# Four small matmul pairs of an mLSTM moved from the heads to the end of the layer, their operands kept in DRAM meanwhile

## The chip, the cores and the metric

The kernel runs on one core of a Trainium2 chip. The metric is device microseconds of one launch, as the median of 3 runs. TensorE (PE) multiplies matrices into PSUM banks, VectorE (DVE), ScalarE (ACT) and GpSimd (POOL) compute on SBUF and PSUM, SyncE (SP) issues DMAs; ACT and POOL issue some too. Each engine executes its instructions in the order in which they stand in its program; between engines semaphores order them.

## The reference

One inference step of one hybrid decoder layer, in float32: 256 prompt tokens and 8 sample tokens (264 columns in all) of width 2048. The part that the change touches is the mLSTM's memory after the prompt, per head (4 heads, key width 128, value width 256):

```python
xn = rmsnorm(x, g_mix);  z = xn @ w_in
q, k, v, logi, logf = ...                    # slices of z
h_ml, C_new, n_new, m_new = mlstm(q, k, v, logi, logf, C0, n0, m0)
# within mlstm, with w_end the weight that each token keeps at the end:
num = ... + jnp.einsum('bhts,bhsv->bhtv', qk, vc)
den = ... + jnp.sum(qk, axis=-1)
C_new = dec[..., None, None] * C + jnp.einsum('bhs,bhsd,bhsv->bhdv', w_end, kc, vc)
n_new = dec[..., None] * n + jnp.einsum('bhs,bhsd->bhd', w_end, kc)
...
x = x + jnp.concatenate([y_rg, y_ml], axis=-1) @ w_out
x = x + o @ w_xa_o                           # cross attention
x = x + (jax.nn.silu(xf @ w_ffn_gate) * (xf @ w_ffn_up)) @ w_ffn_down
y = rmsnorm(x, g_final)
```

For the prompt the old memory is zero, so C_new and n_new are one product: weighted keys (256 tokens x 128) transposed, times values with a column of ones (256 x 257, kept as 258). They are outputs only; nothing later in the layer reads them. The sample tokens have a memory of their own (input c0T, output o_sc), which is read, updated and written back.

## The kernel before

**Weights.** The main loop at the end of layer_kernel walks a list of steps, one for each column block of a weight matrix (w_in, the memory's w_k and w_v, w_out, w_q, w_o, w_gu, w_d in three parts). SP's DMAs bring a step's weights into `raw` (5 buffers of 128x1024, load_piece); ACT rounds them to fp32r and DVE subtracts, which gives a high and a low part in `w` (4 buffers, split_half). PE multiplies each 128x128 chunk three times (high by high, high by low, low by high): 48 matmuls for a step of 16 chunks, 36 in the last part of w_d, which has 12.

**Side work.** Around the weight matmuls run generators that the loop advances (pump): ml_prompt makes each head's masked scores Pm and weighted keys kw, ml_values its values vt, ml_heads the head's sums, ml_sample the update of the sample tokens' memory. A scheduler of the framework then sets each engine's order, except SP's, which is the order of the code.

**The heads.** For each head, ml_heads issues two pairs of matmuls for the output (nps), two for the new memory (cps, 128x258 in a PSUM bank) and three of one column for the denominators (dps, in the same bank behind the memory's columns). ACT copies nps, dps and cps out; cps goes into `cn`, and once all four heads are there POOL writes cn to the output o_pc.

**The sample memory.** ml_sample goes over 4 heads in 8 groups. fetch, called one group ahead, issues three DMAs on POOL's queue: the group's memory from c0T, and two reads that spread rows of a DRAM scratch (`scr`, keys and queries) over all partitions. ACT scales (`dw`), DVE updates and reduces (`ds`), and POOL writes the group to o_sc. POOL issues these in its program's order.

**The end.** The last step's evf is final(15): while PE has no more weights it issues filler matmuls (warm, rows `mm<-ones`); DVE adds the residual, ACT squares, PE sums over partitions (fin_sums, rows `ax<-ones,t`), rstd_fin computes the reciprocal root, PE spreads it to all partitions (spread, rows `ax<-ident,c`), and DVE and POOL scale the 16 blocks of y, which SP and ACT write to o_y in nine DMAs (132 KB a block).

All compute instructions go through the wrapper class Engine, so the profile shows them as line L60; they are told apart by tile names. `B` is a pool of 26 SBUF buffers; PSUM has banks `mm` and `ax`, four each.

Of the kernel before, what the change touches and what calls it, by code (L numbers as in the profile page):

```python
# [10 lines left out]
F32 = mybir.dt.float32  # L11
F32R = mybir.dt.float32r
I32 = mybir.dt.int32
AF = mybir.ActivationFunctionType
# [3 lines left out]
P = 128  # L18
D = 2048
KC = D // P  # L20
T = 256
# [3 lines left out]
H = 4  # L25
# [69 lines left out]
def layer_kernel(ctx: ExitStack, tc, xT, memT, vec, wrg, w_in, w_out, w_q, w_k, w_v, w_o,  # L95
# [3 lines left out]
    act, dve, pe = Engine(nc.scalar, price_act), Engine(nc.vector, price_dve), Engine(nc.tensor, price_pe)  # L99
    pool_e, sp = nc.gpsimd, nc.sync  # L100
# [4 lines left out]
    drm = ctx.enter_context(tc.tile_pool(name="drm", bufs=1, space=bass.MemoryType.DRAM))  # L105
# [8 lines left out]
    def nm(s):  # L114
        uid[0] += 1
        return f"{s}_{uid[0]}"

    def B(shape, dt=F32):
        return sb.tile(shape, dt, tag="B", bufs=NB, name=nm("B"))

    def tmp(w=N, tag="t"):
        t = sb.tile([P, N], F32, tag=tag, bufs=NT if tag == "t" else NL, name=nm(tag))
        return t[:, :w]
# [36 lines left out]
    fin = {}  # L160


    steps = []
# [100 lines left out]
    def halves(x):  # L264

        return x.rearrange("p (b a) -> p b a", b=2)

    def unturn(ps):

        return ps.rearrange("p (a b) -> p b a", b=2)  # L270
# [61 lines left out]
    def bank(tag="mm"):  # L332
        return psm.tile([P, 512], F32, tag=tag, bufs=4, name=nm(tag))
# [3 lines left out]
    def warm(n, w=None):  # L337

        ps = bank()
        for _ in range(n):  # L340
            pe.matmul(ps[:, :P], ones if w is None else w.to_broadcast([P, P]), ones, start=True, stop=True)
# [16 lines left out]
    def ctile(w):  # L358
        t = sb.tile([P, 16], F32, tag="c", bufs=8, name=nm("c"))
        return t[:, :w]  # L360
# [23 lines left out]
    def spread(ps, c, n=N):  # L384

        for j in range(2 if n == T else 3):
            lo, hi = (j * P, j * P + P) if j < 2 else (T, N)
            pe.matmul(ps[:, lo:hi], c[j].to_broadcast([P, P]), ident[:, P - (hi - lo):], start=True, stop=True)
# [48 lines left out]
    def rstd_fin(ps):  # L437
        v, r, t = ctile(3), ctile(3), ctile(3)
        dve.tensor_scalar(v, ps[:, :3], 1.0 / D, EPS, op0=OP.mult, op1=OP.add)
        act.activation(r, v, AF.Sqrt)  # L440
        dve.reciprocal(r, r)
        dve.tensor_mul(t, r, r)
        dve.scalar_tensor_tensor(t, t, -0.5, v, op0=OP.mult, op1=OP.mult)
        dve.scalar_tensor_tensor(r, t, 1.5, r, op0=OP.add, op1=OP.mult)
        warm(3, v[:, 0:1])
        for k in "ps", "copied":
            fin[k] = bank("ax")
            spread(fin[k], [r[:, j: j + 1] for j in range(3)])
        act.activation(rstd, fin["copied"][:, :N], AF.Copy)

    def fin_sums(ps, x, first):

        for j, w0 in enumerate(WIN):
            pe.matmul(ps[:, j: j + 1], x[:, w0: w0 + P], ones[:, 0:1], start=first and j == 0,
                      stop=not first, skip_group_check=True)
# [281 lines left out]
        return f  # L737

    hT = {}

    def ml_prompt():
        qk = ml["qk"]
# [53 lines left out]
            yield STEP  # L796

    def ml_heads():
        cn = B([P, H, 258])
        hT["t"] = Arr(8)  # L800
        hh = hT["t"]
        one = ones[:, 0:1]
        for h in range(H):
            while min(ml.get("pn", 0), ml.get("vtn", 0)) <= h:
                yield STEP
            yield STEP
            vt = ml["vt", h]
            Pm, kw = ml["w", h]
            nps = bank("ax")
            for vb in range(2):  # L810
                o = vb * T
                pe.matmul(nps[:, o: o + T], vt[:, 0, vb * P: vb * P + P], Pm[:, 0:256], start=True, stop=False)
                pe.matmul(nps[:, o + P: o + T], vt[:, 1, vb * P: vb * P + P], Pm[:, 256:384],
                          start=False, stop=True)
            cps = bank("ax")
            pe.matmul(cps[:, 0:258], kw[:, 0:P], vt[:, 0, :], start=True, stop=False)
            pe.matmul(cps[:, 0:258], kw[:, P:T], vt[:, 1, :], start=False, stop=True)
            dps = cps[:, 300:302]
            pe.matmul(dps[:, 0:1], Pm[:, 0:P], one, start=True, stop=True)
            pe.matmul(dps[:, 1:2], Pm[:, P:T], one, start=True, stop=False)  # L820
            pe.matmul(dps[:, 1:2], Pm[:, 256:384], one, start=False, stop=True)
            for vb in range(2):
                act.activation(hh(2 * h + vb)[:, 0:T], nps[:, vb * T: vb * T + T], AF.Copy)
            act.activation(den[:, 3 * h: 3 * h + 2], dps, AF.Abs)
            act.activation(cn[:, h, :], cps[:, 0:258], AF.Copy)
        pool_e.dma_start(o_pc, cn)
        yield STEP

    snew = const.tile([P, H, NS], F32, name="snew")
# [199 lines left out]
    def final(m):  # L1029

        def f(ps):
            x = xres[:, m, :]
            if m == 0:
                st["y"] = Arr(KC)
            if m < KC - 1:
                dve.tensor_add(halves(x), halves(x), unturn(ps[:, :N]))
                sumsq(acc_x, x, m == 0)
            else:
                warm(3)
                sq = tmp()  # L1040
                with tc.high_priority():
                    for b in range(2):
                        xb = halves(x)[:, b, :]
                        dve.tensor_add(xb, xb, unturn(ps[:, :N])[:, b, :])
                        act.activation(halves(sq)[:, b, :], xb, AF.Square)
                fin_sums(fin["sum"], sq, False)
            act.activation(st["y"](m), x, AF.Copy, scale=V("g_final", m))
            if m == 0:
                act.activation(warm_act, acc_x[:, 0:1], AF.Sqrt)
            elif m == KC - 2:  # L1050
                fin["sum"] = bank("ax")
                fin_sums(fin["sum"], acc_x, True)
            elif m == KC - 1:
                rstd_fin(fin["sum"])
        return f
# [380 lines left out]
    kept = ExitStack()  # L1436
    for i, (src, cols, pef, evf, need) in enumerate(steps):
        if i > 1:
            load_piece(i + LD - 1)
        if i == 7:  # L1440
            st["rg"] = side(rg_gen(), 0)
        if "pend" in need:
            with tc.high_priority(300):
                for e, x in pend:
                    e(x)
            pend = []
        for q in need:
            if q in st:
                finish(lambda: st[q].done)
        if not 4 <= i < 7:  # L1450
            with tc.high_priority(300):
                for e, x in pend:
                    e(x)
            pend = []
        now = pe.clock
        dve.clock, act.clock = max(dve.clock, now), max(act.clock, now)
        split_half(i + LS, 0)
        if i + LS < len(steps) and steps[i + LS][1] > 1024:
            split_half(i + LS, 1)
        if i == 4:  # L1460
            kept.enter_context(tc.manual_schedule(engines={mybir.EngineType.PE}))
        ps = pef(i)
        if i == 6:
            kept.close()
        if i == 1:
            with tc.issue_after(st["split"].ins):
                for c in range(8):
                    sumsq(acc_x, xres[:, c, :], c == 0)
        if i == 3:
            with tc.issue_after(st["split"].ins), tc.high_priority():  # L1470
                last_squares()
            st["rstd_x"] = Gen(norm_x())
        if evf is not None:
            pend.append((evf, ps))
        if i == 0:
            for c in range(0, 4, 2):
                load_x(sp, 12 + c, 14 + c)
                load_first(3, c)
                load_first(3, c + 1)
        else:  # L1480
            load_piece(i + LD)
        pump(pe.clock + SLACK)
        if i == 24:
            st["ng"] = side(ml_norm(), 6)
        if i == 57:
            PACE["full"] = False
        if i == 40:
            st["memg"] = side(mem_gen(), 7)
    for e, x in pend:
        e(x)  # L1490
    for lo, hi in ((0, 1), (1, 2), (2, 4), (4, 6), (6, 8), (8, 10), (10, 12), (12, 14), (14, 16)):
        for c in range(lo, hi):
            e, r = (pool_e, rstd) if c in POOLC else (dve, fin["ps"][:, :N])
            e.tensor_mul(st["y"](c), st["y"](c), r)  # L1494
        (act if lo in (1, 4, 8, 12) else sp).dma_start(o_y[:, lo:hi, :], st["y"].tile(lo // 4)[:, lo % 4: lo % 4 + hi - lo, :])


# [104 lines left out]
```

## Time and profile before

| what | value |
|---|---|
| median of 3 runs | 1456.94 us |
| all runs | 1456.13, 1456.94, 1457.64 us |
| profiled execution, time | 1455.83 us |
| profiled execution, span | 1454.1 us |
| granted TensorE clock | 0.998 |
| PE busy | 1439.2 us |
| DVE / ACT / POOL busy | 1045.1 / 794.9 / 128.3 us |
| DMA moved | 326.02 MB, mean 224 GB/s |

The profile is of one execution; the difference between its time and its span, 1.73 us, lies ahead of its first and behind its last instruction or transfer. A row of a timeline gives the start, the duration, the engine, the line, the operation, what it writes and reads, shapes, how many instructions, and in brackets the idle time before it with what ended that. Rows of windows give each engine's busy time, then the granted clock, the DMA engines' busy share and GB/s. f32 matmuls show as several instructions each.

### The profile page before, as it was taken

What the parts mean: (1) busy time and instruction counts of PE and PEld (TensorE: products, weight loads), DVE (VectorE), ACT (ScalarE), POOL (GpSimd) and SP (SyncE); (2) the same over time, 40 slices, a digit from 0 to 9 for tenths busy, and PEclk for the clock granted to TensorE, in tenths of its full rate; (3) what the DMA queues carried; (4) which work ended last, traced back from release to release, by engine and by line L of the source; (5) the groups of instructions that cost most, each with busy time, mean ns of one, the idle gap of its engine ahead of it and who ended that gap; (6) DMA issues with size and microseconds to landing.
All of it is one profiled execution on the core that took longest, in us unless ns stands there. A gap on an engine that the chain in (4) does not pass through costs nothing.

```text
span 1454.1 us, 30126 instructions
## 1 busy us (share of the span) xinstructions
PE 1439.2 (99%) x12071; PEld 1415.5 (97%) x12071; DVE 1045.1 (72%) x1999; ACT 794.9 (55%) x1279; POOL 128.3 (9%) x204
## 2 busy tenths in 40 slices
PE   9999999999999999999999999999999999999997
PEld 8999999999999999999999999999999999999997
DVE  7966797898899999987675666555665655565564
ACT  7678685666556666655544444434444443444463
POOL 0001210000124343410000000000000000000000
PEclk9999999999999999999999999999999999999999
DMA  9645896557799877955555555555555555555563
GB/s 288 234 171 179 268 363 231 177 178 271 254 344 355 340 284 297 375 172 192 197 195 194 197 193 201 190 202 190 198 194 196 196 198 194 195 197 192 172 195 112
DMA packets 99757, 326.02 MB, mean 224 GB/s; under 512 B 10944, under 2 KB 19824, under 8 KB 99616
## 3 DMA queue, kind: packets, MB, share of 16 engines
q1 hardware_dynamic: 83616, 269.84, 52.8%
q0 software_dynamic: 15136, 53.16, 10.2%
q8 instruction: 94, 1.54, 0.4%
q10 hardware_dynamic: 864, 1.09, 0.2%
q14 instruction: 47, 0.39, 0.1%
HBM read 312.78 MB, written 11.28 MB: 223 GB/s over the span
## 4 chain that ended last, share of the span: by engine, by line
PE 94%; ACT 2%; DMA 1%; DVE 1%; issue 1%; SPq 0%; POOL 0%; DVEq 0%; POOLq 0%
PE mm L60 90%; PE ax L60 5%; DMA raw<-w_in 1%; ACT B L60 1%; DVE B L60 1%; DMA B<-scr 0%; ACT w L60 0%; DVE w L60 0%; ACT L60 0%; SPq L213 0%; ACT dw L60 0%; DVE ds L60 0%; SPq L1412 0%; DMA scr<-lt 0%; ACT t L60 0%
## 5 line engine op out<-in xcount | busy, mean ns | idle before, releaser
L60 PE MATMUL mm<-B,w 128*128 128x264 f32 (+1 forms) x10960 | 1281.2, 279 | 2.5 <-DVE w L60 2.1
L60 PEld LDWEIGHTS mm<-B,w 128*128 128x128 f32 x10960 | 1260.6, 189 | 10.7 <-DVE w L60 2.4
L60 DVE TENSOR_TENSOR w<-raw,w 128x1024 fp32r<-128x1024 f32 (+1 forms) x522 | 625.4, 1200 | 312.9 <-ACT w L60 312.2
L60 ACT ACTIVATE w<-raw 128x1024 fp32r<-128x1024 f32 (+1 forms) x522 | 536.0, 1028 | 531.8 <-PE mm L60 370.8
L60 PE MATMUL mm<-w,B 128*128 128x512 f32 x384 | 86.5, 380 | 0.0
L60 PEld LDWEIGHTS mm<-w,B 128*128 128x128 f32 x384 | 70.7, 189 | 9.4
L1494 POOL TENSOR_TENSOR B<-B,rstd 128x264 f32<-128x264 f32 x4 | 2.8, 741 | 802.8 <-ACT rstd L60 802.8
L60 DVE TENSOR_TENSOR t<-mm,rstd 128x264 f32<-128x264 f32 x96 | 41.4, 432 | 28.8 <-PE mm L60 28.7
L60 DVE SCALAR_TENSOR_TENSOR B<-B,dw 128x256 f32<-128x256 f32 x128 | 52.2, 461 | 3.2 <-ACT dw L60 2.9
L60 DVE TENSOR_TENSOR xres<-xres,mm 128x264 f32<-128x264 f32 (+1 forms) x81 | 34.2, 424 | 27.2 <-PE mm L60 27.1
L60 DVE SCALAR_TENSOR_TENSOR dw<-B,qsm,dw 128x256 f32<-128x256 f32 x96 | 48.6, 512 | 0.8
L60 PE MATMUL ax<-B,B 128*128 128x256 f32 (+3 forms) x288 | 46.0, 302 | 0.8 <-DVE B L60 0.8
L1162 POOL TENSOR_TENSOR ds<-dw,ds 128x256 fp32r<-128x256 f32 x32 | 36.8, 1151 | 106.9 <-ACT ds L60 104.7
L60 PEld LDWEIGHTS ax<-B,B 128*128 128x128 f32 x288 | 39.9, 191 | 3.0 <-DVE B L60 1.0
L60 ACT ACTIVATE B<-xres,vecs 128x264 fp32r<-128x264 f32 (+1 forms) x64 | 32.1, 502 | 3.5 <-DVE xres L60 1.6
L60 ACT ACTIVATE t<-xres 128x264 f32<-128x264 f32 (+1 forms) x53 | 21.0, 409 | 16.0 <-DVE xres L60 16.0
L1151 POOL DMA_DIRECT2D B<-kcT x32 | 17.4, 544 | 122.8 <-DVE B L60 109.7
L60 DVE SCALAR_TENSOR_TENSOR B<-xres,vecs,B 128x264 fp32r<-128x264 f32 x48 | 23.3, 488 | 4.3 <-ACT B L60 4.3
L60 ACT ACTIVATE dw<-B,qsm 128x256 f32<-128x256 f32 x32 | 16.2, 507 | 16.3 <-issue 6.4
L60 ACT ACTIVATE B<-t 128x264 fp32r<-128x264 f32 (+1 forms) x60 | 24.1, 409 | 1.7 <-DVE t L60 1.5
L60 ACT ACTIVATE dw<-B,B 128x128 f32<-128x128 f32 x64 | 20.9, 390 | 7.1 <-DMA B<-scr 6.3
L60 ACT ACTIVATE dw<-ax,dw 128x256 f32<-128x256 f32 x32 | 15.0, 470 | 17.7 <-DVE dw L60 14.0
(172 smaller groups left out, 691.2 us busy)
## 6 DMA issues: line engine op xcount, KB each, us to landing
raw<-w_gu SPq DMA_DIRECT2D x176, 512.0 KB, 3.6
raw<-w_d SPq DMA_DIRECT2D x80, 512.0 KB, 3.7
raw<-w_in SPq DMA_DIRECT2D x74, 512.0 KB, 5.2
raw<-w_out SPq DMA_DIRECT2D x32, 512.0 KB, 3.8
B<-kcT POOLq DMA_DIRECT2D x32, 512.0 KB, 8.2
raw<-w_q SPq DMA_DIRECT2D x32, 512.0 KB, 5.4
B<-vcT POOLq DMA_DIRECT2D x32, 512.0 KB, 9.1
raw<-w_k SPq DMA_DIRECT2D x32, 512.0 KB, 5.1
```

The lines of the kernel that those rows point to most:

```text
L60: return f(*a, **k)
L1151: pool_e.dma_start(kc, kcT[h, b])
L1162: pool_e.tensor_sub(ws[:, 1], acc, ws[:, 0].bitcast(F32))
L1494: e.tensor_mul(st["y"](c), st["y"](c), r)
```

## The change

The matmuls for cps leave ml_heads. In their place two POOL DMAs for each head write kw (128 KB) and vt (258 KB) to two DRAM tiles, kept_k and kept_v, and dps gets a bank of its own. ACT's four copies of cps and POOL's write of o_pc leave too.

In the last part of w_d, state_load puts eight loads on SP's queue, between weight loads, which bring keys and values back into three B buffers (a fourth takes the result). The same eight matmuls, two for each head, then stand behind the last weight matmul: the first takes the place of two of three fillers ahead of fin_sums, the next two that of the three fillers ahead of the spreads, the other five follow the spreads. ACT copies the four results (state_out), and SP writes o_pc in two halves of 258 KB, one between two writes of y and one as the last of all. PE's order is that of the code from the last step on.

```diff
@@ rstd_fin
-        warm(3, v[:, 0:1])
+        state_mm((0, 1), (1, 0))
         for k in "ps", "copied":
             fin[k] = bank("ax")
             spread(fin[k], [r[:, j: j + 1] for j in range(3)])
+        state_mm((1, 1))
         act.activation(rstd, fin["copied"][:, :N], AF.Copy)
+        state_out(0, act)
+        state_out(1, act)
+        state_mm((2, 0), (2, 1), (3, 0), (3, 1))
+        state_out(2, act)
+        state_out(3, act)
@@ ahead of ml_prompt
+    kept_k = drm.tile([H, P, T], F32, name="kept_k")
+    kept_v = drm.tile([H, P, 2, 258], F32, name="kept_v")
+
+    def state_load():
+        kb, vb, out = B([P, H, T]), [B([P, 2, 2, 258]), B([P, 2, 2, 258])], B([P, H, 258])
+        for h in range(H):
+            sp.dma_start(kb[:, h], kept_k[h])
+            sp.dma_start(vb[h // 2][:, h % 2], kept_v[h])
+        fin["state"] = kb, vb, out
+        fin["cps"] = {}
+
+    def state_mm(*parts):
+        kb, vb, out = fin["state"]
+        for h, t in parts:
+            if t == 0:
+                fin["cps"][h] = bank("ax" if h % 2 else "mm")
+            pe.matmul(fin["cps"][h][:, 0:258], kb[:, h, t * P: t * P + P], vb[h // 2][:, h % 2, t, :],
+                      start=t == 0, stop=t == 1)
+
+    def state_out(h, engine):
+        out = fin["state"][2]
+        engine.activation(out[:, h, :], fin["cps"][h][:, 0:258], AF.Copy)
@@ ml_heads
-        cn = B([P, H, 258])
...
-            cps = bank("ax")
-            pe.matmul(cps[:, 0:258], kw[:, 0:P], vt[:, 0, :], start=True, stop=False)
-            pe.matmul(cps[:, 0:258], kw[:, P:T], vt[:, 1, :], start=False, stop=True)
-            dps = cps[:, 300:302]
+            pool_e.dma_start(kept_k[h], kw)
+            pool_e.dma_start(kept_v[h], vt)
+            dps = bank("ax")[:, 0:2]
...
-            act.activation(cn[:, h, :], cps[:, 0:258], AF.Copy)
-        pool_e.dma_start(o_pc, cn)
@@ final
-                warm(3)
+                state_mm((0, 0))
+                warm(1)
...
+            elif m == 4:
+                state_load()
@@ main loop and end
+        if i == len(steps) - 1:
+            kept.enter_context(tc.manual_schedule(engines={mybir.EngineType.PE}))
...
+        if lo == 4:
+            sp.dma_start(o_pc[:, 0:2], fin["state"][2][:, 0:2])
         (act if lo in (1, 4, 8, 12) else sp).dma_start(o_y[:, lo:hi, :], ...)
+    sp.dma_start(o_pc[:, 2:4], fin["state"][2][:, 2:4])
```

Three places of the programs show what moves.

POOL, from the write of the last hidden state on, before (c0T and scr are a fetch of the sample memory, o_sc its write; scr's row stands for both halves):

```order
L587 DMA o_h<-hlast 128x72
L896 DMA o_sc<-B_1890 128x1024
L896 DMA o_sc<-B_1985 128x1024
L866 DMA B_2109<-c0T 128x1024
L870 DMA B_2110<-scr 128x512 x2
L896 DMA o_sc<-B_2109 128x1024
L866 DMA B_2320<-c0T 128x1024
```

and now:

```order
L593 DMA o_h<-hlast 128x72
L844 DMA kept_v<-B_1628 256x1x258
L843 DMA kept_k<-B_1890 128x256
L921 DMA o_sc<-B_1891 128x1024
L921 DMA o_sc<-B_1986 128x1024
L844 DMA kept_v<-B_1628 256x1x258
L843 DMA kept_k<-B_1979 128x256
L891 DMA B_2109<-c0T 128x1024
L895 DMA B_2110<-scr 128x512 x2
L843 DMA kept_k<-B_2078 128x256
L844 DMA kept_v<-B_1629 256x1x258
```

The keys and values of two heads stand ahead of the third fetch, the second head's (B_1979) directly ahead of it and behind the two o_sc; those of the third and the keys of the fourth stand ahead of the fourth fetch.

PE at the second head, before (rows of 128x258 are the new memory, rows from `ones` the denominators, mm a weight step):

```order
L60 MATMUL mm_2243<-B_149,w_2122 128x264
L60 MATMUL mm_2243<-B_148,w_2122 128x264 x2
L60 MATMUL mm_2243<-B_149,w_2122 128x264
L60 MATMUL mm_2243<-B_148,w_2122 128x264
L60 MATMUL ax_2205<-B_1626,B_1978 128x258 x2
L60 MATMUL ax_2205<-ones,B_1978 128x1 x3
L60 MATMUL mm_2243<-B_175,w_2122 128x264
```

and now:

```order
L60 MATMUL mm_2242<-B_151,w_2122 128x264
L60 MATMUL mm_2242<-B_150,w_2122 128x264 x2
L60 MATMUL mm_2242<-B_151,w_2122 128x264
L60 MATMUL mm_2242<-B_150,w_2122 128x264
L60 MATMUL ax_2207<-ones,B_1979 128x1 x3
L60 MATMUL mm_2242<-B_177,w_2122 128x264
```

The denominators' matmuls follow the weight matmuls directly; they have a bank of their own (ax_2207) instead of the end of the memory's.

PE at the end, from the last weight matmul on, before (`mm<-ones` are fillers, `ax<-ones,t` the sums, `ax<-ident,c` the spreads):

```order
L60 MATMUL mm_17732<-B_16571,w_17683 128x264
L60 MATMUL mm_17769<-ones 128x128 x3
L60 MATMUL ax_17728<-ones,t_17773 128x1 x3
L60 MATMUL mm_17791<-ones,c_17782 128x128 x3
L60 MATMUL ax_17795<-ident,c_17783 128x128 x2
L60 MATMUL ax_17795<-ident,c_17783 128x8
L60 MATMUL ax_17799<-ident,c_17783 128x128 x2
L60 MATMUL ax_17799<-ident,c_17783 128x8
```

and now, from the first instruction behind the last weight matmul (128x258 rows are the moved matmuls):

```order
L60 MATMUL mm_17779<-B_17211,B_17210 128x258
L60 MATMUL mm_17781<-ones 128x128
L60 MATMUL ax_17736<-ones,t_17783 128x1 x3
L60 MATMUL mm_17779<-B_17211,B_17210 128x258
L60 MATMUL ax_17802<-B_17211,B_17210 128x258
L60 MATMUL ax_17804<-ident,c_17793 128x128 x2
L60 MATMUL ax_17804<-ident,c_17793 128x8
L60 MATMUL ax_17808<-ident,c_17793 128x128 x2
L60 MATMUL ax_17808<-ident,c_17793 128x8
L60 MATMUL ax_17802<-B_17211,B_17210 128x258
L60 MATMUL mm_17816<-B_17212,B_17210 128x258 x2
L60 MATMUL ax_17819<-B_17212,B_17210 128x258 x2
```

Five of six fillers are gone, and of the eight moved matmuls five stand behind the spreads.

More of the change, by code (lines that the diff above doesn't have):

```diff
@@ L1490, in layer_kernel @@
         e(x)
+    kept.close()
     for lo, hi in ((0, 1), (1, 2), (2, 4), (4, 6), (6, 8), (8, 10), (10, 12), (12, 14), (14, 16)):
```

## The prediction

> **What bounds the kernel now.** I read the page first, then every wait of TensorE, then the two stretches that the change edits: the mLSTM heads (150 to 190 us) and the last 14 us.
>
> ```profile
> span 1454.1 us, 30126 instructions
> PE 1439.2 (99%) x12071; PEld 1415.5 (97%) x12071; DVE 1045.1 (72%) x1999; ACT 794.9 (55%) x1279; POOL 128.3 (9%) x204
> PEclk9999999999999999999999999999999999999999
> PE 94%; ACT 2%; DMA 1%; DVE 1%; issue 1%; SPq 0%; POOL 0%; DVEq 0%; POOLq 0%
> ```
>
> PE is busy for 1439.2 of 1454.1 us at full clock, and the chain of waits is 94% PE. A PE instruction taken out therefore shortens the run by what PE issues for it, as long as PE finds the next work ready. The other 15 us lie at the two ends, where a transfer or a short chain decides. In the heads only one wait of PE is seen, the 0.81 us in the first row below.
>
> **What is removed.** Here are PE's rows of the first two heads (start, duration, instructions). The x4 rows of 128x258 are the matmuls that leave; f32 is issued as pieces, four for a head's two matmuls.
>
> ```profile
> 154.50 1.14 PE L60 MATMUL ax<-B,B 128*128 128x258 f32 x4 [0.81 <-DVE B L60]
> 155.48 0.72 PE L60 MATMUL ax<-ones,B 128*128 128x1 f32 x6
> 165.73 1.03 PE L60 MATMUL ax<-B,B 128*128 128x258 f32 x4
> 166.60 0.72 PE L60 MATMUL ax<-ones,B 128*128 128x1 f32 x6
> ```
>
> Durations overlap, so I take start to start: 166.60 - 165.73 = 0.87 us a head. The first shows 0.98, of which I put 0.11 to the restart behind its wait. Four heads: 4 x 0.87 = **-3.48 us**. The four ACT copies and the output's DMA on POOL leave too. I cost them at nothing: ACT waits for PE in most of these gaps, so PE's work covers them. Were the cover gone, that would be worth 4 x 0.38 us (the 156.31 row below is such a copy).
>
> **What the heads add: a longer POOL queue.** Keys and values now leave by POOL DMAs, 128 + 258 KB a head, and a DMA waiting at POOL holds up what is queued behind it. Behind the second head's keys stands the third fetch of the sample state (c0T, then two halves of scr). The rows of POOL and ACT before:
>
> ```profile
> 150.54 0.54 POOL L896 DMA_DIRECT2D o_sc<-B  x1 [7.14 <-DVE ds L60]
> 151.10 0.54 POOL L866 DMA_DIRECT2D B<-c0T  x1
> 151.63 1.08 POOL L870 DMA_DIRECT2D B<-scr  x2
> 154.32 0.39 ACT L60 ACTIVATE B<-B,B 128x128 f32<-128x128 f32 x1
> 156.31 0.38 ACT L60 ACTIVATE B<-ax 128x258 f32<-128x258 f32 x1
> 161.00 1.28 ACT L60 ACTIVATE dw<-B,B 128x128 f32<-128x128 f32 x4 [0.81 <-DMA B<-scr]
> 161.72 1.07 DVE L60 SCALAR_TENSOR_TENSOR B<-B,bcs,dw 128x256 f32<-128x256 f32 x2 [0.27 <-ACT dw L60]
> 163.26 0.74 DVE L60 TENSOR_SCALAR B<-ax,gcol 128x256 f32<-128x256 f32 x2
> ```
>
> The second head's keys are finished by the ACT row at 154.32, thus at 154.71. Their DMA takes one issue slot (0.54), so the fetch starts near 155.3 instead of 151.10: 4.2 us later. It has no slack: ACT at 161.00 already waits 0.81 us for the scr half. Behind ACT stand DVE's state update (161.72) and, in DVE's order, the gate rows ending at 163.26 + 0.74 = 164.00, which free the PSUM bank that PE's second-head sums need.
>
> How much later does scr land? Not the full 4.2 us, if bandwidth rather than issue decides. Two stretches, the first scr read in the chain of waits, and the landings of all of them:
>
> ```profile
> 150.00:155.00 5.00, 4.19 (x28) 3.76 (x27) 5.00 (x20) 2.67 (x7) 2.15 (x4) 1.00 0.85 278
> 155.00:160.00 5.00, 5.00 (x44) 4.92 (x44) 3.78 (x7) 3.77 (x9) 0.00 (x0) 1.00 0.95 301
> 130.03 5.85 DMA B<-scr
> DMA to landing us min/median/max: 1.8/10.1/16.4
> ```
>
> The last two numbers of the windows are DMA share and GB/s. The engines are 85 and 95% busy, so bytes ahead of the fetch decide: 386 KB (0.395 MB) of the second head at 0.278 to 0.301 MB/us is 1.3 to 1.4 us, plus some 0.3 us of idle share that the later issue leaves unused. I take a delay d = **1.7 us**. The bounds: issued at 155.8, with the 5.85 us that the earliest scr read took, it lands at 161.7, against the 161.0 where ACT started (d = 0.7); with the whole issue delay and no help, d = 4.2.
>
> PE now comes to those sums 0.98 us earlier (head one's pieces are gone), at 165.73 - 0.98 = 164.75, and the bank is free at 164.00 + d = 165.7. It stalls 0.95 us: **+0.95**. (d = 0.7 gives no stall, d = 4.2 gives 3.45 us, all of the gain.)
>
> ```profile
> 206.04 1.21 DVE L60 TENSOR_TENSOR w<-raw,w 128x1024 fp32r<-128x1024 f32 x1
> 190.00:200.00 10.00, 10.00 (x91) 10.00 (x91) 10.00 (x44) 9.97 (x30) 1.61 (x3) 1.00 1.02 409
> 200.00:210.00 10.00, 10.00 (x92) 10.00 (x91) 10.00 (x31) 7.62 (x16) 1.60 (x3) 1.00 0.87 334
> ```
>
> From 190 to 210 us DVE is busy all the time, with weight splits like the 1.21 us one among the state updates, and DMA is at a share of 1.02. The four later fetches start some 2 us late, and part of PE's lead meets weights that are not split yet. Against it, 516 KB of output leaves this stretch. I take **+0.2** (0 to 1.5: none if the splits keep their lead, one 1.21 us split and a little if one fetch comes a whole DMA later).
>
> The DMA queues' rows of the window 169 to 176, in which two weight loads were issued, bear on this price:
>
> ```profile
> q0 software_dynamic: 425, 1.51, 86.9%
> q1 hardware_dynamic: 3, 0.01, 0.3%
> raw<-w_in SPq DMA_DIRECT2D x2, 512.0 KB, 12.0
> ```
>
> POOL's queue (q0) had 86.9% of the engines and the weights' queue (q1) 0.3%. So POOL's bytes are served ahead of weights and kept keys and values push weights back in full, which is why I keep an upper end of 1.5. The Trainium skill ("DMA: Bandwidth & Descriptors", "Queues, rings and completion order") says that each engine alternates between the queue rows it has work for, packet by packet; by that, weights would lose about half as much, and the +0.2 would be +0.1. The trace does not agree here.
>
> **What the last layer adds.** The eight loads (1.58 MB) are issued by SP in the last down projection. At 0.39 MB/us they need 4.0 us of all engines, where the share is
>
> ```profile
> 1410.00:1420.00 10.00, 10.00 (x92) 10.00 (x91) 6.02 (x11) 6.33 (x11) 0.00 (x0) 1.00 0.62 192
> 1430.00:1440.00 10.00, 10.00 (x92) 10.00 (x91) 4.62 (x9) 4.17 (x8) 0.00 (x0) 1.00 0.01 2
> ```
>
> 0.62, then 0.01: the weights are all in by 1430, ten microseconds ahead of PE. I cost the loads at **0**, hidden behind that lead; without it, 4.0 us.
>
> The eight matmuls go into PE's gaps at the end (the last row is the landings of y):
>
> ```profile
> 1441.56 0.83 PE L60 MATMUL mm<-ones 128*128 128x128 f32 x6
> 1442.45 0.83 PE L60 MATMUL ax<-ones,t 128*128 128x1 f32 x6
> 1443.54 0.94 PE L60 MATMUL mm<-ones,c 128*128 128x128 f32 x6 [0.25 <-DVE c L60]
> 1444.57 1.50 PE L60 MATMUL ax<-ident,c 128*128 128x128 f32 x12
> 1445.45 4.16 DVE L60 TENSOR_TENSOR B<-B,ax 128x264 f32<-128x264 f32 x12 [0.93 <-PE ax L60]
> 1445.90 4.71 SPq L1495 DMA_DIRECT2D o_y<-B  x5
> 1446.25 3.22 ACTq L1495 DMA_DIRECT2D o_y<-B  x4
> DMA to landing us min/median/max: 1.8/2.3/3.3
> ```
>
> One matmul is 0.87 / 2 = 0.435 us. The first, with one filler where three stood, has 0.89 us (1441.56 to 1442.45); two, 0.87 us, replace the fillers ahead of 1444.57; the other five stand behind the spreads (end 1446.07) and hold up nothing but their own copies, done near 1448.9. **0** on the path, or up to 0.4 if the first pieces crowd the 1442.45 row. ACT's copies of 0.38 us stand between its own y writes, 0 to 0.4 likewise.
>
> What costs is the output's 516 KB, which went out at 192 us and now goes beside y:
>
> ```profile
> 1447.00:1448.00 1.00, 0.00 (x0) 0.00 (x0) 1.00 (x4) 0.00 (x0) 1.00 (x3) 1.00 0.79 282
> 1448.00:1449.00 1.00, 0.00 (x0) 0.00 (x0) 1.00 (x4) 0.00 (x0) 1.00 (x3) 1.00 1.04 393
> 1450.00:1451.00 1.00, 0.00 (x0) 0.00 (x0) 0.00 (x0) 0.00 (x0) 0.00 (x0) 0.50 1.05 401
> 1452.00:1453.00 1.00, 0.00 (x0) 0.00 (x0) 0.00 (x0) 0.00 (x0) 0.00 (x0) 0.50 0.62 239
> ```
>
> From 1448 to 1452.6 the DMA engines are full at 0.39 to 0.40 MB/us while they drain y, after every engine has ended. 0.528 MB / 0.397 = **+1.3 us**. Below: 1.1, since 1447 has 0.2 us of share free; if the span's end were set by something else, 0. Above: 1.8, with another 0.5 us for the last write's landing (y's median less its least, 2.3 - 1.8).
>
> **Sum:** -3.48 + 0.95 + 0.2 + 0 + 1.3 = -1.03. The profiled run took 1455.83 us, 1.73 around its span, and lies 1.11 below the median of 1456.94. So 1455.83 - 1.03 = 1454.8 for a run like it, and 1456.94 - 1.03 = **1455.9** for the median.
>
> **Rivals.** *A, no stall.* If scr lands by 161.7 and the splits keep their lead, -3.48 + 1.3 = -2.2: 1454.8. For it: the landing of 5.85 us. Against: 10.1 is the median of these reads.
>
> *B, the queue at POOL decides (slower).* The place is the second head's keys ahead of the third fetch. If the fetch keeps its 4.2 us and also the 1.3 us of kept bytes, d = 5.5, the stall is 5.5 - 0.75 = 4.75, 1.27 us more than the gain; with the split's 1.5 and the tail's 1.3 that is +4.1: 1461.0. It decides from d = 4.23 on, where stall and removed work cancel. For it: ACT's 0.81 us wait shows no slack at all, and weights get no share while POOL's queue is full. Against: DMA bytes, not issue times, filled 155 to 160.
>
> *C, the tail is cheaper than its bytes.* If the span's end hangs on the last y write's landing rather than on drained bytes, the output hides: 1456.94 - 3.48 = 1453.5. Against: the engines are full to the end.
>
> *D, weights late at the end.* If the 1.58 MB come ahead of weights that PE needs, up to +4.0 - 1.03: 1459.9. Against: the ten idle microseconds at 1430.
>
> That the change does not do what it says I leave out: the matmuls do stand at the end.
>
> **Numbers.** The forecast has 0.47 (own range 1454.6 to 1457.4), A 0.16, C 0.12, B 0.20, D 0.05. A measurement here tells 0.2% (2.9 us) from no change: faster is below 1454.0, slower above 1459.9. C alone is faster, with a little of A's edge: 0.13. Slower are B and half of D: 0.22. The rest, 0.65, is no change. The range 1453.8 to 1460.2 leaves out most of C and the far part of B.
>
> **What would show it.** Right: no 128x258 rows in the heads and 0.87 us less between their neighbours; the third c0T row at POOL near 155.3 and ACT's wait for scr grown from 0.81 to some 2.5 us; one PE wait of about 1 us at the second head's sums; PE's last weight matmul 2.3 us earlier; DMA full 1.3 us longer behind it. A PE wait over 3.5 us there, or PE waits on weight splits between 180 and 220, is B. Weight waits beyond 1400 are D. A drain that is no longer is C. I am wrong altogether if PE's last weight matmul ends later than before, or the tail grows by over 2 us.

## The result, and the profile after

The changed kernel takes 1459.12 us (median of 20 runs, 1456.52 to 1462.48); the kernel before takes 1457.01 us (20 runs, 1455.88 to 1458.47). The ratio is 1.0017, 95% interval 1.001 to 1.0024: 1.5 to 3.5 us slower. The forecast was 1455.9, faster by 1.0.

The profiled execution of the changed kernel took 1461.94 us, at the upper end of its runs. Its page opens with

```profile
span 1460.2 us, 30141 instructions
PE 1442.5 (99%) x12061; PEld 1418.0 (97%) x12061; DVE 1047.2 (72%) x1999; ACT 794.4 (54%) x1279; POOL 133.7 (9%) x211
```

PE issues 10 instructions fewer than before and is still "busy" 3.3 us longer. Busy time grows without work when the clock falls, so the place to look for is one where PE first waits and then runs slowly (it will account for 1.66 of the 3.3 us). The rows of PE in the heads (start, duration, instructions, and in brackets the wait ahead of them):

```profile
153.42 0.59 PE L60 MATMUL ax<-B,ident 128*128 128x256 f32 x2
156.79 0.83 PE L60 MATMUL ax<-ones,B 128*128 128x1 f32 x6 [0.81 <-DVE B L60]
165.72 1.60 PE L60 MATMUL mm<-B,w 128*128 128x264 f32 x12
170.49 1.04 PE L60 MATMUL ax<-ones,B 128*128 128x1 f32 x6 [3.18 <-DVE B L60]
171.39 5.75 PE L60 MATMUL mm<-B,w 128*128 128x264 f32 x36
176.98 1.47 PE L60 MATMUL ax<-B,B 128*128 128x256 f32 x8
178.28 0.73 PE L60 MATMUL ax<-ones,B 128*128 128x1 f32 x6
192.09 43.11 PE L60 MATMUL mm<-B,w 128*128 128x264 f32 x381
```

The 128x258 rows are gone. At the second head's sums PE waits 3.18 us where it had not waited, and the next 36 weight pieces take 5.75 us; they had taken 4.30 (the same row before: `167.19 4.30`). The windows, with the granted clock ahead of the DMA share and GB/s, tell why:

```profile
169.00:171.00 2.00, 0.51 (x5) 0.51 (x5) 2.00 (x11) 2.00 (x6) 0.00 (x0) 0.99 0.01 4
171.00:172.00 1.00, 1.00 (x6) 1.00 (x7) 1.00 (x2) 1.00 (x4) 0.21 (x1) 0.50 0.00 0
173.00:174.00 1.00, 1.00 (x7) 1.00 (x6) 1.00 (x6) 0.46 (x2) 0.56 (x1) 0.50 0.62 156
174.00:175.00 1.00, 1.00 (x9) 1.00 (x9) 0.64 (x5) 0.59 (x1) 0.61 (x2) 0.81 0.92 291
175.00:176.00 1.00, 1.00 (x12) 1.00 (x11) 0.50 (x1) 0.47 (x1) 1.00 (x2) 1.00 0.97 383
```

Behind the wait the clock is a half from 171.0 to 174.4 us. The sums take 0.90 us start to start (170.49 to 171.39) instead of 0.59, the weights 1.45 us more: 1.76 us in all. Of these, 0.10 is the restart behind a wait, which the first head shows at full clock too (156.79 to 157.48, 0.69 us); 1.66 is the clock, a cause that no term of the forecast held.

Who made PE wait? POOL's rows, and those of ACT and DVE behind them:

```profile
152.83 0.54 POOL L921 DMA_DIRECT2D o_sc<-B  x1 [6.83 <-DVE ds L60]
153.36 0.72 POOL L844 DMA_DIRECT2D kept_v<-B  x1
157.28 0.56 POOL L843 DMA_DIRECT2D kept_k<-B  x1 [3.21 <-ACT B L60]
157.83 0.55 POOL L891 DMA_DIRECT2D B<-c0T  x1
158.36 1.08 POOL L895 DMA_DIRECT2D B<-scr  x2
```

```profile
156.60 0.39 ACT L60 ACTIVATE B<-B,B 128x128 f32<-128x128 f32 x1
167.62 1.28 ACT L60 ACTIVATE dw<-B,B 128x128 f32<-128x128 f32 x4 [5.14 <-DMA B<-scr]
169.70 0.74 DVE L60 TENSOR_SCALAR B<-ax,gcol 128x256 f32<-128x256 f32 x2
```

POOL waits 3.21 us for the second head's keys (ACT's row at 156.60) and only then issues the third fetch. ACT waits 5.14 us for scr, DVE's gate rows end at 170.44, and PE starts at 170.49. In this execution all of it runs 2.28 us later than before already ahead of the heads (153.42 against 151.14 for the same PE row). So in the times of before, the fetch starts at 157.83 - 2.28 = 155.55 instead of 151.10, and ACT gets scr at 167.62 - 2.28 = 165.34 instead of 161.00: a delay of 4.3 us, nearly the whole 4.45 us of later issue. (The second profile of the same kernel, e10 below, has 3.3 us.)

Those 2.28 us belong to that execution (e10 has 0.57): 1.8 of them come from the first scr read, for which ACT waited until 138.19 instead of 135.90, and it was issued at 130.83, ahead of the first write of keys or values (143.15).

The end: PE's last weight pieces, before

```profile
1441.14 0.58 PE L60 MATMUL mm<-B,w 128*128 128x264 f32 x3
```

and now, and the windows of the drain.

```profile
1445.45 0.58 PE L60 MATMUL mm<-B,w 128*128 128x264 f32 x3
1446.76 0.83 PE L60 MATMUL ax<-ones,t 128*128 128x1 f32 x6
1448.88 1.50 PE L60 MATMUL ax<-ident,c 128*128 128x128 f32 x12 [0.31 <-DVE c L60]
```

```profile
1451.00:1452.00 1.00, 1.00 (x6) 0.89 (x5) 1.00 (x4) 0.52 (x2) 1.00 (x2) 1.00 0.78 270
1453.00:1454.00 1.00, 0.00 (x0) 0.00 (x0) 0.92 (x3) 0.16 (x1) 0.75 (x2) 1.00 1.02 395
1457.00:1458.00 1.00, 0.00 (x0) 0.00 (x0) 0.00 (x0) 0.00 (x0) 0.00 (x0) 0.89 1.03 398
1458.00:1459.00 1.00, 0.00 (x0) 0.00 (x0) 0.00 (x0) 0.00 (x0) 0.00 (x0) 0.50 0.29 112
```

From the x3 row to the span's end it is 1460.2 - 1445.45 = 14.75 us; before it was 1454.1 - 1441.14 = 12.96. The sums and the spreads stand at the same distances as before (1.31 and 3.43 us), so the moved matmuls cost PE's path nothing; what grew, by 1.79 us, is the drain. (Counted from the last weight instruction, as the expectations below do, it is 0.31 us less: 14.44 and 12.65.)

### The profile page after: what moved, and what is told of

The parts are those of the page before. It is cut to its first block, busy times and chain, and to the rows that moved or that the text cites. A ratio compares the mean times of both kernels' runs of the same rounds, so it can differ in the third digit from the quotient of the medians.

```text
span 1460.2 us, 30141 instructions
## 1 busy us (share of the span) xinstructions
PE 1442.5 (99%) x12061; PEld 1418.0 (97%) x12061; DVE 1047.2 (72%) x1999; ACT 794.4 (54%) x1279; POOL 133.7 (9%) x211
## 4 chain that ended last, share of the span: by engine, by line
PE 68%; DVE 1%; issue 0%; ACT 0%; POOL 0%; DVEq 0%; POOLq 0%; ACTq 0%
PE mm L60 66%; PE ax L60 2%; DVE B L60 0%; DVE w L60 0%; DVE dw L60 0%; POOL ds L1190 0%; ACT w L60 0%; DVE c L60 0%; ACT dw L60 0%; ACT ds L60 0%; DVE osm L60 0%; DVEq L1613 0%; ACT t L60 0%; DVE xres L60 0%; ACT c L60 0%
```

## The experiments

Each was compared with the kernel before on the same chip; ratios are to it.

**e1, the removal alone.** From the change, the writes, the loads, the moved matmuls and o_pc are left out.

```diff
-            pool_e.dma_start(kept_k[h], kw)
-            pool_e.dma_start(kept_v[h], vt)
...
-                state_mm((0, 0))
-                warm(1)
+                warm(3)
```

> The changed kernel without its POOL writes of keys and values, without the loads and without the moved matmuls: the new memory is not computed and o_pc is not written. It prices the removal alone. Theory (POOL's queue delays the third fetch, and only that turns the gain round): the third c0T stands at POOL near its time of before, PE waits under 1 us at the second head's sums, and the run is 2.5 to 3.5 us faster than before (4 x 0.87 us). Rival (the shifted order of ACT and DVE in the heads, not POOL's queue, makes the stall): the wait of about 3 us at the second head's sums stays, and the gain is under 1 us.

Measured: 1453.12 us, ratio 0.9972 (0.9961 to 0.9984), about 4 us faster. PE's rows around the sums of the second head, and the third fetch:

```profile
165.53 0.72 PE L60 MATMUL ax<-ones,B 128*128 128x1 f32 x6
166.11 4.30 PE L60 MATMUL mm<-B,w 128*128 128x264 f32 x36
```

```profile
150.84 0.53 POOL L861 DMA_DIRECT2D B<-c0T  x1
```

No wait, full clock, the fetch in time. PE, DVE and ACT have the changed kernel's order in the heads, so that order isn't what stalls. The removal is worth what the forecast said (3.5 us lies in the interval). That this execution has no 0.81 us wait at the first head is no part of the gain: its clock had fallen earlier, near 127 us, and PE came there late (see e6).

**e2, without the end's part.** The change with its POOL writes, without loads, moved matmuls, copies and o_pc.

```diff
-            elif m == 4:
-                state_load()
...
-    sp.dma_start(o_pc[:, 2:4], fin["state"][2][:, 2:4])
```

> The changed kernel with its POOL writes of keys and values, but without the eight loads, the moved matmuls, their copies and o_pc (which is not written). Against e1 it adds the eight writes alone, against the changed kernel it lacks the tail alone. Theory: the wait of 3 us at the second head's sums and the half clock behind it are there (1.5 to 1.8 us), so it is as fast as before or up to 1.5 us slower; the changed kernel's further 1.3 to 1.8 us is the tail. Rival (the tail costs the whole 2.1 us): 2 us faster than before, like e1.

Measured: 1458.18 us, ratio 1.0012 (1.0003 to 1.002). The wait is there:

```profile
167.82 0.83 PE L60 MATMUL ax<-ones,B 128*128 128x1 f32 x6 [3.20 <-DVE B L60]
```

```profile
169.00:170.00 1.00, 1.00 (x8) 1.00 (x8) 1.00 (x5) 1.00 (x4) 0.68 (x1) 0.71 0.00 0
170.00:171.00 1.00, 1.00 (x6) 1.00 (x6) 1.00 (x7) 0.36 (x2) 0.38 (x1) 0.50 0.67 102
```

Eight POOL writes turn e1's gain of 4 us into a loss of 1.7; that is the larger part of the matter. Between e2 and the change lies the end: 0.0005 of the ratio, which is 0.7 us, with intervals that overlap, and 1.8 us by the profiles' ends (14.75 against 12.92 from the x3 row).

**e3, the writes by SP.** One word in two lines; PE, DVE and ACT keep the changed order.

```diff
-            pool_e.dma_start(kept_k[h], kw)
-            pool_e.dma_start(kept_v[h], vt)
+            sp.dma_start(kept_k[h], kw)
+            sp.dma_start(kept_v[h], vt)
```

> The whole change, with the eight writes of keys and values issued by SP instead of POOL. POOL's order is that of before; PE, DVE and ACT keep the changed kernel's order. Theory: the third fetch is issued in time, the stall at the second head's sums falls under 1 us and the clock stays up; what is left is -3.48 + 1.4 to 1.8 for the tail: 1.5 to 2.2 us faster than before. Rival (bandwidth: 386 KB a head ahead of the fetch, whoever issues it): the wait stays above 2 us and the time is no better than before. A second rival: SP waits for the second head's keys and holds the weights behind them, which shows as PE waits on the weight splits ahead of 190 us.

Measured: 1454.99 us, ratio 0.9989 (0.998 to 0.9998): 1.6 us faster than before, with all of the work done.

```profile
151.24 0.53 POOL L891 DMA_DIRECT2D B<-c0T  x1
```

```profile
160.91 1.28 ACT L60 ACTIVATE dw<-B,B 128x128 f32<-128x128 f32 x4 [0.55 <-DMA B<-scr]
```

The same bytes move in the same stretch (the first head's go out at 150.43, the second head's at 156.24) and scr comes in time; so the bytes were not the price. The read's own time varies, though: in e8, with the same writes by SP, scr came 11.67 us behind its issue instead of 9.15, and PE waited 0.55 us at the second head's sums; whether the bytes do that is not shown. PE shows no wait on weight splits there in e3: SP's own wait for the keys costs nothing.

**e4, the writes by ACT.** As e3, with ACT's queue.

```diff
+            nc.scalar.dma_start(kept_k[h], kw)
+            nc.scalar.dma_start(kept_v[h], vt)
```

> As e3, with the writes issued by ACT, right behind the instructions that make the keys and values. Theory: the third fetch is in time as in e3; eight issue slots of some 0.4 us stand in ACT's order, 3 us in all, mostly while ACT waits for the scr reads: 0.5 to 2.2 us faster than before, not better than e3. Rival: ACT's slots delay weight rounding between 142 and 160 us and PE waits for ACT there: slower than e3 by 1 us or more.

Measured: 1455.09 us, ratio 0.999 (0.9981 to 0.9998), not to be told from e3. ACT's slots cost nothing that these runs show.

**e5, only the second head by SP.**

```diff
+            kq = sp if h == 1 else pool_e
+            kq.dma_start(kept_k[h], kw)
+            kq.dma_start(kept_v[h], vt)
```

> The whole change; only the second head's keys and values are written by SP, the other three heads' by POOL as in the change. Theory (one DMA that waits at POOL ahead of the third fetch is the whole loss): the third c0T is back near 151 to 153 us, PE's wait at the second head's sums is under 1 us, the clock stays at 1.00, and the run is 1 to 2 us faster than before, as e3. Rival (the six other writes cost too, by their slots ahead of the later fetches or by their bytes): between the changed kernel and e3, no faster than before.

Measured: 1455.48 us, ratio 0.9991 (0.9982 to 1.0). The third c0T is issued at 150.68 and PE doesn't wait at the sums. Six of the eight writes may stay on POOL; the two of the second head make nearly all of the difference to the change.

**e6, PE kept busy through the wait.** The second head's output matmuls are done four times.

```diff
-            for vb in range(2):
+            for vb in (0, 1) * (4 if h == 1 else 1):
```

> The changed kernel, with the second head's output matmuls done four times over instead of once (the same result is written again): 24 more PE pieces, 3.7 us by the 1.23 us that eight take, ahead of the sums that PE waits for; 12 pieces of weight matmuls (1.43 us) come behind the sums instead of ahead of them. Theory (the half clock behind the 3.2 us wait is set off by PE's idleness): PE waits under 1.6 us there, the clock stays at 1.00, the next 36 weight pieces take 4.3 instead of 5.75 us, and the added work costs nothing: +1.43 for the pieces moved behind, -1.76 for the clock, 0.3 us faster than the changed kernel or equal to it. Rival (the clock falls there for another reason): it falls again, and the run is 1.2 us or more slower than the changed kernel.

Measured: 1459.86 us, ratio 1.002 (1.0012 to 1.0029), against 1.0017 (1.001 to 1.0024) for the change: 3.7 us of added PE work cost nothing that can be told from the medians.

```profile
162.44 5.40 PE L60 MATMUL ax<-B,B 128*128 128x256 f32 x32
167.99 0.83 PE L60 MATMUL ax<-ones,B 128*128 128x1 f32 x6
168.68 5.65 PE L60 MATMUL mm<-B,w 128*128 128x264 f32 x48
```

```profile
168.00:170.00 2.00, 2.00 (x17) 2.00 (x18) 2.00 (x7) 1.81 (x5) 0.68 (x1) 1.00 0.00 0
170.00:172.00 2.00, 2.00 (x20) 2.00 (x19) 2.00 (x12) 1.13 (x5) 0.99 (x2) 1.00 0.64 158
```

The clock stays at 1.00 and 48 weight pieces take their usual 5.65 us. One profile could be chance, but the clock that is on record for every run says the same: its mean over the run is 0.996 or less in 10 of the change's 20 runs, in 6 of e2's 11 and in 3 of e9's 11, and in none of the 11 of e6, where PE has work at this place. So the fall is due to PE's idleness and not to the place. The gain of 0.3 us over the change that the clock was to bring is too small for these runs; where the clock doesn't fall anyway, the added work costs (the third head's output starts at 174.17 here and at 172.60 in e10).

An earlier wait shows that its length alone doesn't decide. Every profile has PE waiting 1.89 us near 126 us. The first row is the kernel before, the second e6:

```profile
126.52 3.19 PE L60 MATMUL mm<-B,w 128*128 128x264 f32 x26 [1.89 <-DVE w L60]
126.37 4.86 PE L60 MATMUL mm<-B,w 128*128 128x264 f32 x26 [1.89 <-DVE w L60]
```

In e1, e3, e5, e6, e7 and e8 the clock falls behind it and the 26 pieces take 4.8 to 4.9 us; in the other six profiles it doesn't. There the fall costs nearly nothing, since PE then waits less for weight splits and at the first head: its first sums start at 155.20 us in e3 and at 155.08 in e10, which had no fall.

**e7 and e8, the end.** e7 is e3 without the two writes of o_pc. e8 is e3 with two heads finished ahead of the spreads, and their half of o_pc issued ahead of y.

```diff
-                state_mm((0, 0))
-                warm(1)
+                state_mm((0, 0), (0, 1))
...
-        state_mm((0, 1), (1, 0))
+        state_mm((1, 0), (1, 1))
+        state_out(0, act)
...
+        state_out(1, act)
+        sp.dma_start(o_pc[:, 0:2], fin["state"][2][:, 0:2])
         act.activation(rstd, fin["copied"][:, :N], AF.Copy)
...
```

> e3 without the two writes of o_pc (the new memory is computed and copied, and not written out). From PE's last weight matmul to the span's end it was 12.65 us before and 14.45 in e3. Theory (the tail's 1.8 us are the output's bytes): 12.6 to 12.8 again, 1.6 to 1.9 us faster than e3. Rival (the moved matmuls and ACT's copies among the writes of y cost part): 13.1 or more.

> e3 with both matmuls of the first head in the first gap (no filler), both of the second in the second gap, their copies ahead of the spreads' copy, and the first half of o_pc issued by SP ahead of all writes of y, while the DMA engines are idle. Theory: half of the added bytes leave the drain (0.264 MB at 0.397 MB/us = 0.67 us): 13.5 to 13.8 us behind PE's last weight matmul instead of 14.45, 0.7 to 1.0 us faster than e3, thus about 2.7 us faster than before. Rival (ACT's two copies delay the root or the first y): 14.4 or more, no faster than e3.

Measured: e7 1453.4 us, ratio 0.9978 (0.9969 to 0.9987); e8 1454.93 us, ratio 0.9985 (0.9976 to 0.9993). Their spans are 1451.5 and 1453.4 us, and their last weight pieces, e7's and then e8's,

```profile
1438.50 0.58 PE L60 MATMUL mm<-B,w 128*128 128x264 f32 x3
```

```profile
1439.41 0.58 PE L60 MATMUL mm<-B,w 128*128 128x264 f32 x3
1442.97 0.34 SPq L451 DMA_DIRECT2D o_pc<-B  x1
```

leave 13.00 and 13.99 us to the end; in e3 it is 14.76 (1453.4 - 1438.64), before 12.96. With the writes away the end is back at its old length, so the moved matmuls and copies cost nothing there and the two writes all of the 1.8 us. Half of them issued early saves 0.77. By its ratio e8 is the fastest kernel here that does all of the work, faster than the kernel before and than the change; from e3 it can't be told.

**e9, a wait without bytes.** e1 with one DMA of 1 KB that waits for the second head's keys, ahead of the third fetch. The other four engines have e1's order.

```diff
+            if h == 1:
+                pool_e.dma_start(kept_k, kw[0:1, :])
```

> e1 (no new memory, o_pc not written) with one DMA added at POOL ahead of the third fetch: 1 KB of the second head's weighted keys to DRAM, which waits for ACT as the change's second head does. PE, DVE, ACT and SP keep e1's order. Theory (the wait at the head of POOL's queue is the loss, not the bytes): the third c0T is issued 4 us later than in e1, PE waits about 3 us at the second head's sums, the clock falls to a half behind it, and the run is 4.5 to 5.5 us slower than e1: 0.5 to 1.5 us slower than before. Rival (bytes): 1 KB moves nothing, the run is as fast as e1, 3.5 to 4 us faster than before.

Measured: 1457.86 us, ratio 0.9999 (0.999 to 1.0008), against e1's 0.9972 (0.9961 to 0.9984): 0.27%, 3.9 us, for 1 KB. A little less than was expected.

```profile
155.82 0.50 POOL L817 DMA_DIRECT2D kept_k<-B  x1 [3.91 <-ACT B L60]
156.32 0.56 POOL L864 DMA_DIRECT2D B<-c0T  x1
```

```profile
168.30 0.83 PE L60 MATMUL ax<-ones,B 128*128 128x1 f32 x6 [2.44 <-DVE B L60]
168.99 5.96 PE L60 MATMUL mm<-B,w 128*128 128x264 f32 x36
```

```profile
171.00:172.00 1.00, 1.00 (x6) 1.00 (x6) 1.00 (x7) 0.83 (x3) 0.90 (x2) 0.50 0.85 262
```

This settles it: what POOL waits for at the head of its queue is the loss, not what it carries.

**e10, the change once more.** No edit.

> The changed kernel once more, for a second profile. Theory: the wait of 3.2 us at the second head's sums, the half clock behind it and the 14.4 us from PE's last weight matmul to the end are there again; the 1.76 us by which the first profile's first scr read was later than before need not be. Rival (the wait is a matter of that one execution): under 2 us.

Measured: one run of 1458.33 us, span 1456.6.

```profile
167.77 0.83 PE L60 MATMUL ax<-ones,B 128*128 128x1 f32 x6 [2.17 <-DVE B L60]
168.46 4.30 PE L60 MATMUL mm<-B,w 128*128 128x264 f32 x36
```

```profile
207.58 24.34 PE L60 MATMUL mm<-B,w 128*128 128x264 f32 x214 [0.49 <-DVE w L60]
```

```profile
164.90 1.28 ACT L60 ACTIVATE dw<-B,B 128x128 f32<-128x128 f32 x4 [4.14 <-DMA B<-scr]
```

The wait is 2.17 us here, less than expected though over the rival's 2, and behind it the weights take 4.30 us: the clock did not fall. At 207.58 PE waits once more, 0.49 us for a weight split. ACT has scr at 164.90; less the 0.57 us by which this execution is late at the second head's keys (154.89 against 154.32), that is 3.3 us later than before. The end takes 14.78 us from the x3 row, as in the first profile.

The two profiles' spans differ by 3.6 us. Behind the fourth head it is 4.38 (192.09 against 187.71): 1.71 stood there ahead of the heads, 1.22 came at the second head's wait and sums, and 1.45 is the slow clock on the weights; later on e10 loses 0.75 more than the first. Do such falls of the clock explain why the change's runs spread over 6 us where those before spread over 2.6? In large part: of the seven runs above 1461 us six are among the ten with a mean clock of 0.996 or less, no run of e1 and e3 to e8 is so low, nor one of the kernel before among those that its ratios rest on, and e6, with PE kept busy, spreads over 2.8 us only. The profiled run itself (1461.94 us, mean clock 0.998) shows that the clock is not all of it.

## Why the prediction was wrong

*What is removed: -3.48 us.* Right. The gaps of 0.87 us are gone, and e1, which has nothing else, gains 4 us with an interval of 2.3 to 5.7.

*The third fetch is issued near 155.3.* Right: 155.55 in the times of before.

*"so bytes ahead of the fetch decide ... I take a delay d = 1.7 us".* This step failed. The forecast read a DMA share of 0.85 and 0.95 as a full pipe, in which a later issue mostly means a shorter time in the queue. The read took about as long as before, so most of the issue delay came through: d = 4.3 in the first profile, 3.3 in e10, 3.5 in e9. e3 and e9 show it from both sides: with all of the bytes and no wait ahead, PE loses nothing at these sums in e3, and 1 KB with the wait costs 3.9 us. The shares were right and the conclusion was not: what stood in the engines in those microseconds was for the most part other work (from 152 to 161 us of the change the weights' queue had 61.5% of them, POOL's 27.7%), and the fetch's own time behind its issue shrank by 0.1 us in the first profile and by 1.1 in e10. The bound of 4.2 stood in the text, with the whole gain as its price; I chose the wrong end.

*The stall: d - 0.75 = 0.95.* The chain was right link by link (POOL, scr, ACT, DVE's gate rows, the bank, PE), only its size was wrong: with d = 4.3 the same formula gives 3.5, and PE waited 3.18 us; with e10's 3.3 it gives 2.6, and PE waited 2.17.

*No term for the clock.* A second failing. The forecast costed a stall at its own length. In the first profile it cost 3.18 + 1.76, in e10 2.17 and a restart. The Trainium skill ("TensorE: Matmul & The Clock Gate", "Why this matters for your kernels") warns of PE-idle gaps over about 3 us, behind which the clock drops to half. The traces agree for the waits of 3.18 us (the change) and 3.20 us (e2), but show no such limit: the clock fell behind 2.44 us in e9 and behind the 1.89 us near 126 us in six of the twelve profiles, and didn't behind 2.17 us in e10. The half clock lasted 3.413 us all nine times. The full-clock stretch ahead of it is a whole multiple of that in each trace (122.88 us, 36 times, in e1, e3, e5 and e6; 163.84 us, 48 times, in e2 and e9). So what may decide is where a wait falls against a grid of 3.413 us; no run here tests it.

*The later fetches: +0.2.* Within its bounds of 0 to 1.5, but not shown to be what was meant: behind the fourth head the weights start 3.91 us later than before (192.09 against 188.18), at the end 4.31 (1445.45 against 1441.14), 0.4 more. The same 0.4 stands in e3, whose fetches are in time (1253.35 us between these two points, 1252.96 before), and in e9, which writes 1 KB; what it comes from stays open. In e10 a weight split came 0.49 us late at 207.58, in the stretch that was named. The reading behind the upper end, that POOL's bytes always go ahead of weights, holds in the window shown and not beyond it: from 180 to 185 us of the same profile POOL's queue had 52.2% of the engines and the weights' 46.8%.

*The loads: 0.* Right: PE shows no wait in the last down projection.

*The end: +1.3.* The mechanism was right, the size low: 1.79 in the first profile, 1.7 to 1.8 in the six with both writes last. (The engines had not all ended by 1448, as the forecast says: DVE and POOL worked until about 1449.6. The DMA engines were full from 1448 all the same.) Some 1.4 of it is drained bytes by the windows' shares; the other 0.4 lies between the end of the transfers and the end of the span. Why it is longer there stays open.

*The rivals.* B is what happened, by the mechanism and the place that it named, though of the signs that it was given the wait over 3.5 us did not come (3.18 and 2.17), and a wait on a weight split came in e10 alone. "It decides from d = 4.23 on" is misread: there the stall cancels the removed work alone. With the forecast's own +0.2 and +1.3 the sum turns positive from d = 2.73 on, so a delay like e10's 3.3 leaves no gain either. B's 1461.0 was too high since it added 1.3 us of kept bytes to the delay and 1.5 us of weights, which cost next to nothing. The sum by what the first profile measured: -3.48 + 3.18 + 1.76 + 0.4 + 1.79 = +3.65; its span is 6.1 us longer than the one before, of which 2.28 stood ahead of the heads, which leaves 3.8. Where the clock doesn't fall it is less; the medians say +2.1.

## What to carry to other kernels

Ahead of each DMA that an edit puts into an issuing engine's order, read what it waits for and what is queued behind it: here one kilobyte that waited 4 us for a result delayed the prefetch behind it by 4 us. Put such writes on a queue whose next transfer has slack (here SP or ACT instead of POOL), or behind the prefetch (not tried here). And give a TensorE wait of about 2 us or more a chance of the slow clock behind it: 1.66 us each time it came at the second head, unless PE would have waited again soon after.

## What the hardware showed that was not expected

Little of a later issue was caught up while the DMA engines were 85 to 100% busy: from the issue of the scr reads to ACT's start on them it was 9.4 us before (151.63 to 161.00) and 9.3 in the change (158.36 to 167.62). Over all profiles it was 8.3 to 9.3 us in the five with the late fetch and 9.0 to 11.7 in the seven others. The same 1.89 us wait of TensorE halved the clock in six profiles and not in six. And 3.7 us of repeated matmuls (e6), where the change waits for 3.2, kept the clock up and cost nothing that the medians show.
